# Moving layer two's memory attention to its beginning, twelve gates to its end, and eight state updates into the output stage

## The chip, the cores and the metric

The kernel runs on one core of one Trainium2 chip. A core has a matmul engine (TensorE, PE in the profile, with PEld for its weight loads), VectorE (DVE), ScalarE (ACT), GpSimd (POOL) and SyncE (SP), each with its own instruction queue, and 16 DMA engines that the queues of SP and POOL feed here. An engine runs its queue strictly in order. The metric is device time in microseconds (us) of one execution.

## What is computed

The reference is one inference step of a two-layer decoder trunk for 256 prompt tokens and 8 sample tokens (264 columns in all), width 2048. Layer one is sliding-window attention, layer two a gated linear recurrence (HGRN2) with 12 heads of key size 128 and value size 128. Each layer also has 4 memory heads. Both layers end in the same way:

```
branch = concatenate([mix, mem_o]) * silu(g)      # 12 mixer heads + 4 memory heads, 16 x 128
y = einsum('bte,ed->btd', branch, w_out_i)
return layer_norm(alpha * h + y)
```

In layer two the projection of the 264 tokens gives, for each head, a query q, a forget gate f and a value v, then 4 memory queries and 16 gate blocks g. For the prompt the recurrence runs over the tokens; for a sample token there is one step from a cached 128x128 state per head:

```
fg = lb + (1 - lb) * sigmoid(f);  k = 1 - fg;  q = silu(q)
o     = q . (fg * state) + (q . k) v
state = fg * state + k v^T                        # an output, per sample and head
o = o * rsqrt(mean(o^2) + eps) * norm_w
```

The memory heads attend to 256 memory rows: for the prompt, rows that the kernel projects itself, for each sample a cached set of keys and values (8 samples x 4 heads).

## The kernel before

All data stand with features on the 128 partitions and tokens in the free dimension. Every operand of a projection is split into two fp16 parts, a high and a low one, and a product is three matmuls (high-high, high-low, low-high: `passes`, L302 to L305). A 128-wide block of a projection (`proj`, L307) is thus 16 x 3 = 48 matmuls with 264 columns.

The program is a list of **units** (class `Stream`, L58). Most are a 1 MB block of weights (or of a cache) that SP loads into one of four `raw` slots (L79), ACT turns into its high half (L97), DVE into its low half (L98), in one of four `hl` slots; then the unit's function runs on PE. The loader and the splits run up to four units ahead. A unit that is not split, or is marked `whole`, keeps its raw slot until its own function has used it. Beside the list there is a queue of **sides**: generators for the work between projections, of which `pump(1)` advances the first by one step after each unit. A scheduler then fixes the order on each engine from the written order, its priorities and its own estimate of durations; an engine does not leave that order on the chip.

Names that the text below uses:

- `f`, `hv`, `hq`, `mq`, `g`, `o` are the outputs of projections: forget gate, value, query, memory query, gate, and output block.
- `hg_side` (L1064 to L1195) is the prompt's recurrence for a pair of heads. It runs over seven levels (1, 2, 4 up to 64): at each, ACT and DVE prepare a pair of split operands (L1079, L1080, L1084), PE makes products `hs` (12 matmuls), DVE keeps them under a mask (L1111). At the end come the transposes `pk` (L1152), ACT's copies `st` (L1147) and `kn` (L1154), the products `pu` (L1158) and `hpo` (L1169 to L1171), and the normalization: ACT squares, PE sums (`rms`, L1182), ACT takes a logarithm and an exponential with a table load before each (L1183, L1186), and DVE writes the head's `mix` (L1189). A gate (`gate_by`, L727 to L730) multiplies it by silu(g) and splits it for the output projection.
- `state_unit` (L1197) is the sample step of one head: eight small products with the cached state (`hos`), and the **state update**: eight matmuls `vb` (L1233) that spread the sample's v over the partitions, eight ACT scalings in place (L1237) and eight DVE multiply-adds in place (L1238), then POOL stores the 512 KB (L1241).
- `ck_unit`, `cv_unit` (outputs `mss`, `mso`) are the samples' memory attention, one unit per two samples for keys and for values; `memp_side` is the prompt's.

Layer two stands in this order: six pairs of heads, each with units f, f, v, v, q, state, q, state; in the first four pairs each head's gate follows its state unit (eight early gates, `NG1 = 8`); then four mq units; then the eight cache units with gates between them, the rest of the eight late gates; then 16 output units `o`. The first eight output units run over all 264 columns. The last eight have `held` slots of their own for the split weights and run over 176 columns first; the other 88 columns follow after the last of them, and then the final layer norm.

## Time and profile before

| what | value |
|---|---|
| runs | 905.26 us median of three (904.99 to 907.28) |
| profiled execution | 906.08 us, its span 904.3 us, granted TensorE clock 0.994 of full |
| PE busy | 886.6 us (98% of the span) |
| DVE busy | 701.5 us (78%) |
| ACT busy | 582.4 us (64%) |
| POOL busy | 34.9 us (4%) |
| DMA | 198.67 MB, 220 GB/s on average |

The span is from the first to the last instruction of one execution; the 1.8 us between it and that execution's time lie around it. PE counts as busy while a matmul is in flight, also when it runs at a lower clock, so a stage loses time in two ways: where PE is not busy, and where the granted clock is below 1. "Idle before, releaser" in a row is the time that the engine stood before that instruction and what ended it. For a group of instructions "busy us, mean ns" gives the union of their times and the mean of one. An instruction's own duration contains a fixed part that overlaps with the next one on the same engine, so the busy time divided by the count is what one of a row of them costs its engine.

### The profile page before, as it was taken

The page shows a single profiled execution, that of the slowest core. Times are in us where ns is not written, and L with a number is a line of the kernel's source. Part 1 is how long each engine was busy: PE and PEld are TensorE (multiplying, and loading weights), DVE is VectorE, ACT ScalarE, POOL GpSimd, SP SyncE. Part 2 cuts the span into 40 slices and gives each one's busy share as a digit, 9 for nine tenths or more (in the row PEclk, how much of TensorE's full clock was granted, in tenths as well). Part 3 has the DMA queues.
Part 4 walks back from the last instruction along what each step waited for, and adds up shares of the span by engine and source line. Part 5 has one row for each costly group of instructions (what it writes and reads, how often), then busy time and mean ns, then how long its engine had stood idle before and what let it go on. Part 6 is the DMA issues. An engine that isn't in the chain of part 4 may idle for free.

```text
span 904.3 us, 21814 instructions
## 1 busy us (share of the span) xinstructions
PE 886.6 (98%) x9281; PEld 762.9 (84%) x9281; DVE 701.5 (78%) x1230; ACT 582.4 (64%) x982; POOL 34.9 (4%) x68
## 2 busy tenths in 40 slices
PE   9999999999999999999999999999999999799996
PEld 6888889678888888876888888898888888688996
DVE  6879877669886666697687887979788989678736
ACT  6767776657664444476766877777777585858415
POOL 1100010000000000002000000000000000000000
PEclk9999999999999999999999999999999999899999
DMA  9998566557785555556374655827454878456303
GB/s 340 392 353 317 188 245 209 188 208 265 262 333 192 187 192 203 207 198 214 127 292 137 216 201 174 299 101 260 160 215 164 303 283 308 172 207 244 130 2 97
DMA packets 37853, 198.67 MB, mean 220 GB/s; under 512 B 4555, under 2 KB 10732, under 8 KB 17532
## 3 DMA queue, kind: packets, MB, share of 16 engines
q1 hardware_dynamic: 33024, 181.55, 56.3%
q0 software_dynamic: 4688, 15.67, 4.6%
q8 instruction: 72, 1.18, 0.5%
q14 instruction: 25, 0.20, 0.1%
q10 hardware_dynamic: 44, 0.07, 0.0%
HBM read 180.03 MB, written 17.22 MB: 218 GB/s over the span
## 4 chain that ended last, share of the span: by engine, by line
PE 77%; DVE 8%; ACT 6%; DMA 6%; issue 3%; SPq 0%; ACTq 0%; DVEq 0%
PE o L303 5%; PE o L305 5%; PE o L304 5%; PE g L305 5%; PE g L303 5%; PE g L304 5%; DVE hl L98 4%; ACT hl L97 2%; PE hv L305 2%; PE hv L303 2%; PE hv L304 2%; DMA raw<-in_w_in 2%; PE hq L303 2%; PE hq L305 2%; PE hq L304 2%
## 5 line engine op out<-in xcount | busy, mean ns | idle before, releaser
L98 DVE SCALAR_TENSOR_TENSOR hl<-raw,hl 128x2048 f16<-128x2048 f32 (+2 forms) x168 | 358.6, 2138 | 82.0 <-ACT hl L97 81.0
L97 ACT ACTIVATE hl<-raw 128x2048 f16<-128x2048 f32 (+2 forms) x168 | 299.2, 1784 | 97.8 <-PE o L305 45.4
L305 PEld LDWEIGHTS <-hl 128*128 128x128 f16 (+2 forms) x2048 | 197.4, 98 | 31.8 <-DVE hl L98 2.9
L303 PEld LDWEIGHTS <-hl 128*128 128x128 f16 (+2 forms) x2048 | 197.3, 98 | 30.6 <-issue 2.2
L304 PEld LDWEIGHTS <-hl 128*128 128x128 f16 (+2 forms) x2048 | 197.4, 98 | 30.3 <-issue 2.2
L305 PE MATMUL g<-xhl,hl 128*128 128x264 f16 x512 | 142.0, 277 | 2.4 <-DVE hl L98 2.4
L303 PE MATMUL g<-xhl,hl 128*128 128x264 f16 x512 | 141.9, 277 | 0.0
L304 PE MATMUL g<-xhl,hl 128*128 128x264 f16 x512 | 141.9, 277 | 0.0
L303 PE MATMUL o<-mix,hl 128*128 128x264 f16 x384 | 105.4, 276 | 0.8 <-DVE xres L747 0.8
L304 PE MATMUL o<-mix,hl 128*128 128x264 f16 x384 | 105.8, 276 | 0.0
L305 PE MATMUL o<-mix,hl 128*128 128x264 f16 x384 | 105.7, 276 | 0.0
L303 PE MATMUL q<-xhl,hl 128*128 128x264 f16 x192 | 53.0, 276 | 1.0 <-DVE kst L251 1.0
L303 PE MATMUL f<-xhl,hl 128*128 128x264 f16 x192 | 52.9, 276 | 0.4 <-DVE mvhl L251 0.4
L305 PE MATMUL hv<-xhl,hl 128*128 128x264 f16 x192 | 53.0, 276 | 0.0
L303 PE MATMUL hq<-xhl,hl 128*128 128x264 f16 x192 | 53.0, 276 | 0.0
L304 PE MATMUL hq<-xhl,hl 128*128 128x264 f16 x192 | 53.0, 276 | 0.0
L305 PE MATMUL hq<-xhl,hl 128*128 128x264 f16 x192 | 53.0, 276 | 0.0
L304 PE MATMUL hv<-xhl,hl 128*128 128x264 f16 x192 | 53.0, 276 | 0.0
L303 PE MATMUL hv<-xhl,hl 128*128 128x264 f16 x192 | 53.0, 276 | 0.0
L304 PE MATMUL q<-xhl,hl 128*128 128x264 f16 x192 | 53.0, 276 | 0.0
L305 PE MATMUL q<-xhl,hl 128*128 128x264 f16 x192 | 53.0, 276 | 0.0
L304 PE MATMUL f<-xhl,hl 128*128 128x264 f16 x192 | 52.9, 276 | 0.0
(338 smaller groups left out, 1858.4 us busy)
## 6 DMA issues: line engine op xcount, KB each, us to landing
raw<-in_w_in SPq DMA_DIRECT2D x88, 1024.0 KB, 6.4
raw<-in_w_o SPq DMA_DIRECT2D x32, 1024.0 KB, 5.0
raw<-in_w_mk SPq DMA_DIRECT2D x8, 1024.0 KB, 4.9
raw<-in_w_mv SPq DMA_DIRECT2D x8, 1024.0 KB, 4.9
raw<-in_c_mk SPq DMA_DIRECT2D x8, 1024.0 KB, 5.1
raw<-in_c_mv SPq DMA_DIRECT2D x8, 1024.0 KB, 7.0
raw<-in_state SPq DMA_DIRECT2D x12, 512.0 KB, 5.4
out_ss<-raw POOLq DMA_DIRECT2D x12, 512.0 KB, 5.5
```

The costliest lines, as they stand in the source:

```text
L97: hi = self.nc.scalar.activation(hl[:, 0, s], raw[:, s], AF.Copy, scale=scale)
L98: lo = self.nc.vector.scalar_tensor_tensor(hl[:, 1, s], raw[:, s], scale, hl[:, 0, s], op0=ALU.mult, op1=ALU.subtract)
L303: mm(out, lhs(0), rhs(0), start=start, stop=False)
L304: mm(out, lhs(0), rhs(1), start=False, stop=False)
L305: return mm(out, lhs(1), rhs(0), start=False, stop=stop)
```

## The change

- The four memory queries and the eight cache units come right behind the first f unit of layer two, mixed with the units of the first pair of heads. The prompt's memory attention is queued behind the last memory query.
- A pair has one state unit for its two heads, behind both q units. It loads the pair's 1 MB, and its small operations (products with q, their splits, the sum) run once for the pair. The factor 1/(SA*SK), which one DVE operation per head applied, is put into the constant `sel`.
- Early gates remain for heads 0, 2, 3 and 6. The other twelve come after the last pair, heads 10 and 11 at the very end.
- Heads 4 to 11 no longer update their state in the state unit. That unit stores what the update needs (v, fg and k, 320 bytes per partition and head) to DRAM (`kept`). Behind the output units 0, 2, 4 up to 14 stands an **update unit** each: it loads the head's 512 KB of state a second time, with its kept piece, into a raw slot, updates it and stores it. It isn't split, so it keeps its raw slot until its store has been made.
- From the first pair's state unit on, sides advance by two steps per unit where more than one waits.

The core of the diff:

```diff
--- before.py
+++ after.py
@@ -31,7 +31,8 @@
-NG1 = 8
+EARLY = (0, 2, 3, 6)
+LATER = tuple(range(4, HD))
...
+KEPT = P // 2 + 2 * TS
...
         n = 4 if i == 0 else 2 if i < 4 else 1
-        w = self.units[i][0].shape[1] // n
+        src = self.units[i][0]
+        if isinstance(src, list):
+            return [None]
+        w = src.shape[1] // n
         return [slice(k * w, (k + 1) * w) for k in range(n)]
 
     def load(self, i):
         t = self.pool.tile([P, 2048], F32, tag="raw", name=f"raw{i}", bufs=self.nraw)
         for k, s in enumerate(self.parts(i)):
+            if s is None:
+                for home, src in self.units[i][0]:
+                    self.nc.sync.dma_start(home(t), src)
+                continue
             self.nc.sync.dma_start(t[:, s], self.units[i][0][:, s])
             if i < 4:
                 self.after_load(i, k)
...
+    kept = {pi: dp.tile([P, 2, KEPT], F32, name=f"kept{pi}") for pi in sorted({h // 2 for h in LATER})}
...
-            nc.vector.tensor_scalar_mul(ks8, kk, 1.0 / (SA * SK))
...
-            scaled = mix[:, h] if h >= NG1 else sq
+            scaled = sq if h in EARLY else mix[:, h]
...
+    def update(h, R, vr, fgs, ks, sel):
+        for g in range(2):
+            pvb = bank("pt", 2, f"vb{h}{g}")
+            for bb in range(4):
+                mm(pvb[:, bb * P : (bb + 1) * P], sel[:, 4 * g + bb], vr, start=True, stop=True)
+            for bb in range(4):
+                b = 4 * g + bb
+                s = R[:, b]
+                nc.scalar.activation(s, s, AF.Copy, scale=fgs[:, b : b + 1])
+                nc.vector.scalar_tensor_tensor(
+                    s, pvb[:, bb * P : (bb + 1) * P], ks[:, b : b + 1], s, op0=ALU.mult, op1=ALU.add
+                )
+        nc.gpsimd.dma_start(ss_o[h // 2, :, h % 2 * TS * P : (h % 2 + 1) * TS * P], R.rearrange("p b v -> p (b v)"))
...
+    def update_unit(h):
+        def fn(raw):
+            if not late_sel:
+                late_sel.append(cp.tile([P, TS, P], F16, tag="ms", name="late_sel", bufs=2))
+                nc.sync.dma_start(late_sel[0], sel_d)
+            R = raw[:, : TS * P].rearrange("p (b v) -> p b v", b=TS)
+            k = raw[:, TS * P : TS * P + KEPT]
+            update(h, R, k[:, : P // 2].bitcast(F16), k[:, P // 2 : P // 2 + TS], k[:, P // 2 + TS :], late_sel[0])
+
...
+    def state_unit(pi):
         def fn(hl):
             p1 = H["p"]
-            pi, i = h // 2, h % 2
...
+            raw = stream.raw[state_at[pi]]
+            v = hl.rearrange("p s (i b v) -> p s i b v", i=2, b=TS)
+            vr, fgs, ks = cur["vr"], cur["fg"][:, :, TP:T], cur["kk"]
+            qs, vts = (cur[n][:, :, TP:T] for n in ("q", "vt"))
...
+            qkh = p1.tile([P, 2, 2, TS], F16, tag="qkh", name=f"qkh{pi}", bufs=2)
+            split_from(qfh[:, :, :, 0], qfh[:, :, :, 1], qf, 1.0)
+            split_from(qkh[:, 0], qkh[:, 1], qk, 1.0)
+            po = bank("ms", 1, f"hos{pi}")
+            pov = po[:, : 4 * TS].rearrange("p (i b s) -> p i b s", i=2, s=2)
+            for i in range(2):
+                for b in range(TS):
+                    mm(pov[:, i, b], v[:, 0, i, b], qfh[:, i, b], start=True, stop=False)
+                    mm(pov[:, i, b, 0:1], v[:, 1, i, b], qfh[:, i, b, 0:1], start=False, stop=True)
+            pq = po[:, 4 * TS : 6 * TS]
             for s in range(2):
-                mm(pq, H["ones"], qkh[:, s], start=s == 0, stop=s == 1)
+                mm(pq, H["ones"], qkh[:, s].rearrange("p i b -> p (i b)"), start=s == 0, stop=s == 1)
             nc.vector.tensor_reduce(qf, pov, axis=AX.X, op=ALU.add)
...
-            for g in range(2):
-                pvb = bank("pt", 2, f"vb{h}{g}")
-                for bb in range(4):
-                    mm(pvb[:, bb * P : (bb + 1) * P], H["sel"][:, 4 * g + bb], vr, start=True, stop=True)
-                for bb in range(4):
-                    b = 4 * g + bb
-                    s = R[:, b]
-                    nc.scalar.activation(s, s, AF.Copy, scale=fgs[:, b : b + 1])
-                    nc.vector.scalar_tensor_tensor(
-                        s, pvb[:, bb * P : (bb + 1) * P], ks8[:, b : b + 1], s, op0=ALU.mult, op1=ALU.add
-                    )
-            nc.gpsimd.dma_start(ss_o[pi, :, i * TS * P : (i + 1) * TS * P], raw)
+            nc.vector.tensor_tensor(qk, pq.rearrange("p (i b) -> p i b", i=2), vts, op=ALU.mult)
+            nc.vector.scalar_tensor_tensor(osb[pi][:, :, TP:T], qf, 1.0 / (SA * SA), qk, op0=ALU.mult, op1=ALU.add)
+            if 2 * pi in LATER:
+                tail = vr[:, :, P // 2 :]
+                nc.vector.tensor_copy(tail[:, :, :TS], fgs)
+                nc.vector.tensor_copy(tail[:, :, TS:], ks)
+                nc.gpsimd.dma_start(kept[pi], vr)
+                return
+            R = raw.rearrange("p (i b v) -> p i b v", i=2, b=TS)
+            for i in range(2):
+                update(2 * pi + i, R[:, i], vr[:, i, : P // 2].bitcast(F16), fgs[:, i], ks[:, i], H["sel"])
 
         return fn
 
...
+    w1("f", 0, f_unit(0))
+    for h in range(NM):
+        w1("mq", h, mem1_sides(mq_unit(h)) if h == NM - 1 else mq_unit(h))
+    cache(c_mk, ck_unit, 0)
+    w1("f", 1, f_unit(1))
+    cache(c_mk, ck_unit, 1)
+    cache(c_mk, ck_unit, 2)
+    w1("v", 0, hv_unit(0))
+    cache(c_mk, ck_unit, 3)
+    w1("v", 1, hv_unit(1))
+    w1("q", 0, hq_unit(0))
+    cache(c_mv, cv_unit, 0)
+    cache(c_mv, cv_unit, 1)
+    gate_of(0)
+    cache(c_mv, cv_unit, 2)
+    cache(c_mv, cv_unit, 3)
+    w1("q", 1, hq_unit(1))
+    state_of(0)
+    for pi in range(1, HD // 2):
         for part, unit in (("f", f_unit), ("v", hv_unit)):
             for i in range(2):
-                stream.add(wb(w_in1, NB1[part] + 2 * pi + i), unit(2 * pi + i))
+                w1(part, 2 * pi + i, unit(2 * pi + i))
+        w1("q", 2 * pi, hq_unit(2 * pi))
+        w1("q", 2 * pi + 1, hq_unit(2 * pi + 1))
+        state_of(pi)
         for h in (2 * pi, 2 * pi + 1):
-            stream.add(wb(w_in1, NB1["q"] + h), hq_unit(h))
-            state_at[h] = len(stream.units)
-            stream.add(state[pi][:, (h % 2) * TS * P : (h % 2 + 1) * TS * P], state_unit(h), SA, whole=True)
-            if h < NG1:
-                stream.add(wb(w_in1, NB1["g"] + h), early_gate(h))
-    for h in range(NM):
-        stream.add(wb(w_in1, NB1["mq"] + h), mq_unit(h))
-
...
-    def g1(j):
-        stream.add(wb(w_in1, NB1["g"] + j), gate_unit(1, j))
-
-    late = deque(range(NG1, NC))
-    for n, (c, unit, t) in enumerate([(c_mk, ck_unit, t) for t in range(4)] + [(c_mv, cv_unit, t) for t in range(4)]):
-        stream.add(c[1, t], unit(1, t), SA)
-        if late and (late[0] < NQ or n == 7 or late[0] < NQ + 2 and n > 3):
-            g1(late.popleft())
-    while late:
-        g1(late.popleft())
+            if h in EARLY:
+                gate_of(h)
+    last = (HD - 2, HD - 1)
+    for j in [j for j in range(NC) if j not in EARLY and j not in last] + list(last):
+        gate_of(j)
     for i in range(NC):
         stream.add(wb(w_o[1], i), out_unit(1, i), home=hold if i >= NC - NSPLIT else None)
+        if i % 2 == 0 and i // 2 < len(LATER):
+            h = LATER[i // 2]
+            srcs = [
+                (lambda t: t[:, : TS * P], state[h // 2][:, (h % 2) * TS * P : (h % 2 + 1) * TS * P]),
+                (lambda t: t[:, TS * P : TS * P + KEPT], kept[h // 2][:, h % 2]),
+            ]
+            stream.add(srcs, update_unit(h), split=False)
...
-        pump(1)
+        pump(2 if len(side) > 1 and i > state_at[0] else 1)```

What stands on the engines at three places follows, the names as in the code, the numbers behind a name being the unit or the head. First, ACT at the end of the last pair's recurrence. Before:

```order
L97 ACTIVATE hl153_10922<-raw153_10651 128x2048
L1147 ACTIVATE st5_10088<-hs5_64_10507 64x4x64
L1154 ACTIVATE kn5_10526<-pk5_10521 128x512
L1162 ACTIVATE s15_10570<-pu5_10565 128x256
L672 ACTIVATE mrows1_10690,mrz1_10692<-mrow1_10687,mrnm1_10691 32x256
```

In the changed kernel, same place:

```order
L106 ACTIVATE hl155_11053<-raw155_11046 128x2048
L1087 ACTIVATE qk16_2_5659<-qk32_10_9550 128x2x4x64
L1155 ACTIVATE st5_10129<-hs5_64_10544 64x4x64
L1213 ACTIVATE raw157_11050<-raw157_11050 128x128 x7
L1162 ACTIVATE kn5_10563<-pk5_10558 128x512
L1213 ACTIVATE raw157_11050<-raw157_11050 128x128
L1170 ACTIVATE s15_10631<-pu5_10626 128x256
```

Seven scalings of head 6's state (raw157, an update unit's slot) have moved between the copies `st` and `kn`; the split of a weight block (hl155, output unit 3) stands ahead of `st`.

Second, PE at the same moment. Before, with the memory softmax and the gates behind it:

```order
L1152 MATMUL pk5_10521<-ident_66,qk32_10_9379 128x128 x4
L1169 MATMUL hpo5_10636<-st5_10088,vn10_9535 128x128
L1170 MATMUL hpo5_10636<-st5_10088,vn10_9535 128x128
L1158 MATMUL pu5_10565<-vn10_9535,kn5_10526 128x128 x4
L666 MATMUL mrow1_10687<-ident_66,mst1_10685 32x128 x2
...
L677 MATMUL mback1_10698<-ident_66,mrows1_10690 128x32 x2
L1182 MATMUL rms50_10704<-osq50_10644,ones_rms_81 128x264
L1182 MATMUL rms51_10707<-osq51_10646,ones_rms_81 128x264
```

In the changed kernel:

```order
L315 MATMUL o11_0_11056<-mix_99,hl152_10895 128x264
...
L1160 MATMUL pk5_10558<-ident_66,qk32_10_9550 128x128 x4
L1177 MATMUL hpo5_10697<-st5_10129,vn10_9705 128x128
L1178 MATMUL hpo5_10697<-st5_10129,vn10_9705 128x128
L1166 MATMUL pu5_10626<-vn10_9705,kn5_10563 128x128 x4
...
L1209 MATMUL vb50_11167<-raw154_10782,late_sel_11017 128x128
L1190 MATMUL rms50_10769<-osq50_10705,ones_rms_81 128x264
L1190 MATMUL rms51_10772<-osq51_10707,ones_rms_81 128x264
...
L1209 MATMUL vb61_11328<-raw157_11050,late_sel_11017 128x128
...
L313 MATMUL o10_0_10964<-mix_99,hl150_10779 128x264
```

The end of the recurrence has moved into the output stage (o10 and o11 are layer two's output units 0 and 1): 30 matmuls of each unit, its first ten of 16 blocks, stand ahead of it; from `pk` on only `hpo`, `pu`, `rms` and the 24 `vb` of three updates (heads 4, 5 and 6) follow, and then the output units' blocks 10 to 15, of which blocks 10 and 11 are this very pair's.

Third, SP's loads in the output stage. Before:

```order
L79 DMA raw161_11165<-in_w_o 128x2048
L79 DMA raw162_11241<-in_w_o 128x2048
L79 DMA raw163_11301<-in_w_o 128x2048
L79 DMA raw164_11367<-in_w_o 128x2048
L79 DMA raw165_11426<-in_w_o 128x2048
```

In the changed kernel:

```order
L88 DMA raw155_11046<-in_w_o 128x2048
L88 DMA raw156_11048<-in_w_o 128x2048
L86 DMA raw157_11050<-in_state 128x1024
L86 DMA raw157_11050<-kept3_94 128x80
L88 DMA raw158_11194<-in_w_o 128x2048
L88 DMA raw159_11196<-in_w_o 128x2048
L86 DMA raw160_11198<-in_state 128x1024
L86 DMA raw160_11198<-kept3_94 128x80
```

Between two blocks of weights each there is now a state with its kept piece, in the same queue and out of the same four raw slots.

61 lines of the change are left out of this document (24 added, 37 removed).

## The prediction

> **What bounds the kernel now.** I read the page's busy times first, then layer two stage by stage, then the timeline of the one stage that loses time.
>
> ```profile
> PE 886.6 (98%) x9281; PEld 762.9 (84%) x9281; DVE 701.5 (78%) x1230; ACT 582.4 (64%) x982; POOL 34.9 (4%) x68
> core 0: us, PE busy (x) PEld busy (x) DVE busy (x) ACT busy (x) POOL busy (x), PEclk, DMA share, GB/s
> 420.00:725.00 305.00, 304.64 (x3218) 269.81 (x3218) 251.97 (x489) 219.48 (x390) 14.69 (x27) 1.00 0.58 206
> 750.00:775.00 25.00, 22.33 (x253) 19.22 (x250) 22.31 (x28) 14.03 (x18) 0.40 (x1) 1.00 0.76 275
> 775.00:800.00 25.00, 22.17 (x264) 18.32 (x265) 20.39 (x37) 20.64 (x39) 0.15 (x1) 0.86 0.58 220
> 800.00:825.00 25.00, 24.70 (x221) 21.46 (x220) 17.04 (x25) 15.94 (x21) 0.00 (x0) 1.00 0.43 158
> 825.00:850.00 25.00, 24.52 (x233) 21.54 (x231) 23.27 (x20) 16.77 (x13) 0.00 (x0) 1.00 0.70 259
> ```
>
> PE bounds: in the recurrence's stage (420 to 725) it stands 0.36 us of 305, though DVE is busy for 83% of it. The losses are in the 50 us behind: 2.67 + 2.83 us of idle, and a clock of 0.86 over 25 us, worth 0.14 x 25 = 3.5 us. **That is 9.0 us; the output stage to 850 loses 0.30 + 0.48 = 0.8.** Taking DVE or ACT work out of 420 to 725 gains at most 0.4 us.
>
> The 9 us are the end of the last pair's recurrence, a chain from engine to engine:
>
> ```profile
> 769.31 0.63 PE L1152 MATMUL pk<-ident,qk 128*128 128x128 f32 x4
> 771.06 0.36 ACT L1147 ACTIVATE st<-hs 64x256 f32<-64x256 f32 x1
> 771.32 0.58 ACT L1154 ACTIVATE kn<-pk 128x512 f32<-128x512 f32 x1
> 771.47 0.49 PE L1169 MATMUL hpo<-st,vn 128*128 128x128 f32 x2 [1.53 <-ACT st L1147]
> 774.93 0.57 ACT L1173 ACTIVATE osb<-hpo 128x512 f32<-128x512 f32 x1
> 776.41 1.28 ACT L1183 ACT_TABLE_LOAD   x1
> 778.58 1.28 ACT L1186 ACT_TABLE_LOAD   x1
> 780.33 0.90 DVE L1189 SCALAR_TENSOR_TENSOR mix<-osb,small_t,osq 128x264 f32<-128x264 f32 x2 [3.67 <-ACT osq L1186]
> ```
>
> From `kn` to the end of the last `mix` it takes 781.23 - 771.32 = 9.9 us. Little independent PE work stood beside it.
>
> **Part by part.** Prices of what moves, and the spacing of PE's products:
>
> ```profile
> L1237 ACT ACTIVATE raw<-raw,fg 128x128 f32<-128x128 f32 x96 | 29.5, 391 | 3.5 <-DVE hl L98 3.5
> L1238 DVE SCALAR_TENSOR_TENSOR raw<-vb,ks,raw 128x128 f32<-128x128 f32 x96 | 26.7, 345 | 0.2 <-PE vb L1233 0.2
> L97 ACT ACTIVATE hl<-raw 128x2048 f16<-128x2048 f32 x69 | 131.3, 1905 | 25.5 <-DMA raw<-in_w_in 6.7 <-PE g L305 6.4 <-issue 3.8
> L98 DVE SCALAR_TENSOR_TENSOR hl<-raw,hl 128x2048 f16<-128x2048 f32 x69 | 158.0, 2292 | 23.9 <-ACT hl L97 23.4
> 808.44 0.28 PE L305 MATMUL o<-mix,hl 128*128 128x264 f16 x1
> 808.55 0.28 PE L303 MATMUL o<-mix,hl 128*128 128x264 f16 x1
> 854.79 0.24 PE L303 MATMUL o<-mix,held 128*128 128x176 f16 x1
> 854.86 0.24 PE L304 MATMUL o<-mix,held 128*128 128x176 f16 x1
> 721.92 0.39 PE L1169 MATMUL hpo<-st,vn 128*128 128x128 f32 x2
> 722.14 0.39 PE L1233 MATMUL vb<-vr,sel_t 128*128 128x128 f16 x4
> 722.37 0.44 PE L1170 MATMUL hpo<-st,vn 128*128 128x128 f32 x2
> 779.76 0.17 PE L696 MATMUL mso<-msphl,hl 128*128 128x2 f16 x1
> 779.78 0.17 PE L697 MATMUL mso<-msphl,hl 128*128 128x1 f16 x1
> ```
>
> One update costs ACT 8 x 29.5/96 = 2.5 us, DVE 8 x 26.7/96 = 2.2 us and PE 8 x 0.23/4 = 0.46 us. A block costs PE 48 x 0.1125 = 5.4 us at 264 columns (0.11 between starts) and 48 x 0.076 = 3.65 us at 176. An fp32 product starts every 0.11 us.
>
> *Sample steps by pairs.* 12 small products fewer at about 0.025 us: **-0.3 us**. Some 40 DVE and 20 ACT operations on 8 or 16 columns go too; they lay under PE work (the 304.64 of 305), so nothing. The updates of heads 4 to 11 leave that stage: 64 x 0.28 = 18 us of DVE and 20 us of ACT, again covered by PE.
>
> *Memory attention first.* Same products, same splits, a place without any recurrence beside it. The changed order runs the 128 value products `mso` in one go, 128 x 0.025 = 3.2 us, and behind them stands a projection whose split queues behind the last cache split: ACT 1.9 and twice DVE 2.29 make 6.5 us, from a slot that comes free about when `mso` starts. So PE waits 0 (slots free earlier) to 3 us. **+1.0 us**, nearer the low end, since transposes and an update's products stand between.
>
> *Twelve gates last.* They were to lie beside the last pair's recurrence, but in the order shown the end of the recurrence stands behind the first 60 matmuls of output units 0 and 1, and nothing but its own products and 24 `vb` stands behind it. Blocks 10 and 11 of the output projection are that pair's. So PE must stand through the chain again. From `pk`:
> - `kn` waits for seven scalings of head 6's state (7 x 0.31 = 2.15 us), and these for that state's load, issued once DVE has split output unit 3 out of the same slot. Three DVE operations, about 1.5 us, lie between that split and `pk`. State loads take:
>
> ```profile
> DMA to landing us min/median/max: 3.8/5.4/7.3
> ```
>
>  With 0.3 us for SP's issue the state lands 2.6 to 4.2 us after `pk`, or has landed if PE comes late. `kn` then starts 0.65 + 2.15 = 2.8 to 6.4 us after `pk`; I take 4.6, the middle. (Before: 2.0, behind a weight split.)
> - From `kn` to `mix` 9.9 us, less about 0.8 for the memory softmax's operations, which stood in that chain and are gone: 9.1.
> - Then the gate, three operations of 0.43, and four multiply-adds of an update ahead of it (1.1): 2.4.
>
> Sum 16.1 us. PE's own work in it: 24 fp32 products of 0.11 (2.6), `rms` 0.9, 24 `vb` 1.4, together 4.9. Idle 11.2 us (9.4 to 13.0). The clock cost 3.5 us around the old gap; for the new I take 2.0 (0 to 3.5), since `vb` lies spread through it. 13.2 us against 9.0: **+4.2 us** (+0.4 to +7.5).
>
> [...]
>
> *Updates in the output stage.* Their ACT and DVE time fits (for two blocks of 10.8 us DVE has 2 x 2.29 + 2.2 and some 2.5 of sums). The four raw slots are the question. Rows for the weight loads of this stage and for the stores of a state, from issue to landing:
>
> ```profile
> DMA to landing us min/median/max: 4.8/5.0/6.8
> DMA to landing us min/median/max: 2.9/5.5/7.4
> ```
>
> A state holds its slot until PE has come to its `vb` and the store has landed. Call R the moment at which PE resumes. PE then has 36 matmuls of units 0 and 1 (4.05 us) and five blocks (27) before head 7's `vb`: R+31.5. Update with other work about 3.2: R+34.7; store 5.5: R+40.2; in its slot the load of output unit 12, 5.0, and its split, 1.9 + 2.29: R+49.4; in that slot unit 13, again 9.2: R+58.6, where PE needs it at R+56.5 (one more wide block, five narrow ones, three updates' `vb`). In that slot head 11's state lands at R+64.0; its eight scalings stand on ACT ahead of unit 15's split (2.5 + 4.2): R+70.7, where PE needs unit 15 at R+64.25. So 6.4 us late with medians, and 1.8 with the fastest rows (2.9, 4.8, 3.8). I take the middle, 4.1, less the 0.8 that the stage loses now: **+3.3 us** (+1.0 to +5.6). The stores' traffic itself (8 states read again, 4 MB) isn't the bound: this stage's DMA share was 0.43 and 0.70.
>
> **Sum**: -0.3 + 1.0 + 4.2 + 3.3 = +8.2 us on the profiled execution's 906.08: 914.3; that execution is 0.8 us above the median of the runs: **913.5 us**.
>
> **Rivals.**
> 1. *The chain runs bare (faster).* Place: ACT between `st` and `kn`, decided by head 6's state landing before `pk`. Summing the chain's own rows instead of its distances, `kn` 0.6, `pu` 1.1, copy 0.4, `hpo` 1.1, 0.6, 0.7, table 1.3, 0.9, table 1.3, 0.4, `mix` 0.9 and gate 1.3 give 10.6; with 0.65 + 2.15 ahead 13.4, less PE's 4.9: 8.5, and `vb` keeps the clock up. And the loader's lead of up to eight held blocks takes the output stage's 0.8 to 0, the recurrence's 0.4 goes: 8.5 - 9.0 - 0.8 - 0.4 - 0.3 = -2.0; if two of the links overlap by another 1.5, -3.5: **902 us**. For it: ACT has slack there. Against: the 9.9 us measured is the longer reading, and the slot order above.
> 2. *The gap only moves (no change).* The gap's 9.4 with a clock as now or better, loads at their fastest: +0.4 + 1.0 - 0.3: **906 us**. For it: the same chain made the old gap.
> 3. *The recurrence lags PE's order throughout (much slower).* A late pair now has six blocks, 32.4 us, and some 8 us of its own products per pass, but
>
> ```profile
> 493.57 0.44 PE pk L1152 x4
> 545.25 0.49 PE pk L1152 x4
> ```
>
>  one pass took 51.7 us with eight blocks. If passes need 45 us instead of 40.4, four of them cost 18 us: **925 us**. Against: DVE loses 18 us of updates there, and the order keeps a recurrence running behind several units.
>
> **Chances.** Forecast (907 to 921) 0.60; rival 1 0.18; rival 2 0.15; rival 3 0.07. The forecast's own range is the sum of the bounds, 906.5 to 921; toward rival 1 the range goes to 901. What a measurement of this kernel can tell from no change is about 0.3%, 2.7 us: faster 0.18, same 0.18, slower 0.64.
>
> **What would show it.** In the new profile the old losses at 750 to 800 are gone from the gates' stage; PE stands some 10 us in `hpo` and the first resumed `o`, released by ACT `kn` and DVE L740, with a clock below 1 around it; ACT L1213 waits for in_state; late `o<-mix,held` rows wait for DVE L107 behind in_w_o. It is wrong if that gap is under 7 us, if no held block waits, or if `hs` products wait over 5 us in the pairs' stage.

## The result and the profile after

| kernel | runs | ratio to before |
|---|---|---|
| before | 905.48 us median of four (904.99 to 907.28) | |
| after | 920.43 us median of four (918.53 to 922.76) | 1.0157, 95% interval 1.0136 to 1.0179 |

The change makes the kernel 14 us slower (0.0157 x 905.48 = 14.2). The forecast was slower, 913.5 us, with a range of 901 to 921. The profiled execution of the changed kernel took 922.76 us, its span 921.0 us, 16.7 us more than the 904.3 before. That execution is the slowest of the four, 2.3 us above their median.

The page's busy times come first:

```profile
PE 894.4 (97%) x9269; PEld 768.2 (83%) x9269; DVE 696.3 (76%) x1178; ACT 581.7 (63%) x964; POOL 37.2 (4%) x72
```

PE is busy 7.8 us longer than before (894.4 against 886.6) with twelve instructions fewer, and idle 8.9 us longer (921.0 - 894.4 = 26.6, against 904.3 - 886.6 = 17.7). So about half of the loss is idle time, and the other half is the same products at a lower clock (0.984 of full over the span, against 0.994). The windows (width, then busy time of PE, PEld, DVE, ACT and POOL, then the granted clock) show where, first after and then before:

```profile
475.00:500.00 25.00, 24.39 (x298) 20.73 (x297) 18.33 (x19) 17.10 (x27) 0.00 (x0) 0.86 0.67 232
700.00:840.00 140.00, 130.95 (x1262) 112.81 (x1261) 102.47 (x177) 90.53 (x147) 4.32 (x8) 0.96 0.49 169
840.00:895.00 55.00, 50.52 (x576) 48.17 (x574) 38.37 (x83) 25.73 (x47) 2.67 (x5) 0.94 0.57 211
```

```profile
475.00:500.00 25.00, 25.00 (x269) 22.27 (x267) 19.58 (x33) 16.47 (x37) 0.00 (x0) 1.00 0.43 153
700.00:840.00 140.00, 134.16 (x1458) 116.50 (x1456) 117.65 (x177) 95.41 (x122) 2.15 (x4) 0.98 0.70 255
840.00:895.00 55.00, 54.52 (x851) 53.10 (x850) 31.60 (x71) 20.06 (x45) 0.00 (x0) 1.00 0.15 51
```

Idle time plus (1 - clock) x width is what a stage loses. (The clock is printed to 0.01, so the figure is good to 0.7 us over 140 us and to 0.3 over 55.)

| stage | before | after | more |
|---|---|---|---|
| memory attention first, 475 to 500 | 0 | 0.6 + 3.5 = 4.1 | 4.1 |
| end of the last recurrence, 700 to 840 | 5.8 + 2.8 = 8.6 | 9.0 + 5.6 = 14.6 | 6.0 |
| held output blocks, 840 to 895 | 0.5 | 4.5 + 3.3 = 7.8 | 7.3 |

The three sum to 17.4, against 16.7 in the spans. Each has its chain of rows.

**The end of the last recurrence.** PE's timeline and ACT's in the changed kernel:

```profile
797.72 0.63 PE L1160 MATMUL pk<-ident,qk 128*128 128x128 f32 x4
802.04 1.46 PE L1166 MATMUL pu<-vn,kn 128*128 128x128 f32 x8 [2.98 <-ACT kn L1162]
814.16 0.60 PE L313 MATMUL o<-mix,hl 128*128 128x264 f16 x2 [3.99 <-ACT mix L739]
```

```profile
799.36 2.15 ACT L1213 ACTIVATE raw<-raw 128x128 f32<-128x128 f32 x7 [1.06 <-DMA raw<-kept]
801.41 0.57 ACT L1162 ACTIVATE kn<-pk 128x512 f32<-128x512 f32 x1
811.38 0.90 DVE L1197 SCALAR_TENSOR_TENSOR mix<-osb,small_t,osq 128x264 f32<-128x264 f32 x2 [0.61 <-ACT osq L1194]
```

`kn` comes 3.7 us behind `pk`. ACT first waits for head 6's kept piece, then does its seven scalings. From the start of `kn` to the start of `mix` it takes 10.0 us, and from there to the first resumed product of output unit 0 another 2.8: 16.4 us from `pk`, with little for PE to do.

**The held output blocks.** SP's waits between 820 and 900, then DVE's timeline, then PE's:

```profile
SPq L86 <- DMA out_ss<-raw: 8.4, 1, 8.4
SPq L88 <- DMA out_ss<-raw: 6.2, 1, 6.2
```

```profile
848.57 2.29 DVE L107 SCALAR_TENSOR_TENSOR held<-raw,held 128x2048 f16<-128x2048 f32 x1
857.72 2.29 DVE L107 SCALAR_TENSOR_TENSOR held<-raw,held 128x2048 f16<-128x2048 f32 x1 [2.69 <-ACT held L106]
859.92 0.42 DVE L757 SCALAR_TENSOR_TENSOR xres<-xres,o 128x264 f32<-128x264 f32 x1
885.51 2.29 DVE L107 SCALAR_TENSOR_TENSOR held<-raw,held 128x2048 f16<-128x2048 f32 x1 [1.45 <-ACT held L106]
```

```profile
860.40 0.24 PE L313 MATMUL o<-mix,held 128*128 128x176 f16 x1 [2.33 <-DVE xres L757]
887.87 0.25 PE L315 MATMUL o<-mix,held 128*128 128x176 f16 x1 [2.00 <-DVE held L107]
```

Loads wait 6.2 and 8.4 us for a state's store to leave its raw slot. By the ring of slots, three of the four held the states of heads 7, 8 and 9, so the weights of output units 10 and 11 went one after the other through the fourth: the split of unit 10 ended at 850.86, unit 11's load was issued at 850.89. Its split stood on DVE from 857.72 for 2.29 us, and the sum of output unit 7 (`xres`), next in DVE's order, started behind it at 859.92. That sum empties the accumulation bank that output unit 9 needs: PE stood 2.33 us, though unit 9's own weights had long been split. At 887.87 output unit 15 waits for its own split.

**The clock.** The stretches that the trace shows at half clock, three of them with the 3.41 us ahead:

```profile
485.32:488.73 3.41, 3.41 (x108) 3.38 (x106) 1.53 (x1) 3.41 (x5) 0.00 (x0) 1.00 0.51 216
488.73:495.56 6.83, 6.22 (x64) 4.61 (x61) 6.83 (x8) 5.26 (x5) 0.00 (x0) 0.50 0.71 217
802.75:806.16 3.41, 3.36 (x21) 2.97 (x19) 1.64 (x6) 0.46 (x2) 0.26 (x1) 0.50 0.00 0
812.99:819.82 6.83, 5.66 (x26) 3.74 (x26) 2.21 (x7) 1.36 (x3) 0.53 (x1) 0.50 0.94 350
857.37:860.78 3.41, 1.07 (x18) 0.95 (x16) 3.03 (x3) 0.65 (x2) 0.00 (x0) 1.00 0.65 223
860.78:864.19 3.41, 3.41 (x27) 3.41 (x25) 3.29 (x13) 2.28 (x3) 0.00 (x0) 0.50 0.68 254
884.67:888.08 3.41, 1.26 (x17) 0.88 (x15) 2.56 (x3) 1.05 (x2) 0.00 (x0) 1.00 0.02 7
888.08:891.50 3.42, 3.42 (x27) 3.42 (x25) 2.80 (x11) 0.35 (x1) 0.53 (x1) 0.50 0.00 0
```

Each of the two windows of 3.41 us in which PE was busy 1.07 and 1.26 us is followed by one at half clock. So was the one ahead of 488.73, in which PE was busy throughout, 97 of its 108 products having one or two columns. The rows at 802.75 and 812.99 belong to the end of the last recurrence. In the first, products of the chain itself run at half clock and fill time in which PE would have waited; in the second, the resumed products of the output units do, and there the slow clock costs time.

### The profile page after: what moved, and what is told of

It is laid out like the page before. It is cut to its first block, busy times and chain, and to the rows that moved or that the text cites. A ratio compares the mean times of both kernels' runs of the same rounds, so it can differ in the third digit from the quotient of the medians.

```text
span 921.0 us, 21766 instructions
## 1 busy us (share of the span) xinstructions
PE 894.4 (97%) x9269; PEld 768.2 (83%) x9269; DVE 696.3 (76%) x1178; ACT 581.7 (63%) x964; POOL 37.2 (4%) x72
## 4 chain that ended last, share of the span: by engine, by line
PE 85%; ACT 5%; DMA 4%; DVE 4%; SPq 1%; issue 0%; ACTq 0%
PE g L313 6%; PE g L314 6%; PE g L315 6%; PE o L313 5%; PE o L315 5%; PE o L314 5%; PE f L313 2%; PE q L313 2%; PE f L314 2%; PE f L315 2%; PE q L315 2%; PE q L314 2%; PE hv L315 2%; PE hv L314 2%; PE hv L313 2%; PE hq L313 2%
## 5 line engine op out<-in xcount | busy, mean ns | idle before, releaser
L107 DVE SCALAR_TENSOR_TENSOR hl<-raw,hl 128x2048 f16<-128x2048 f32 (+2 forms) x162 | 357.6, 2210 | 100.6 <-ACT hl L106 99.8
L106 ACT ACTIVATE hl<-raw 128x2048 f16<-128x2048 f32 (+2 forms) x162 | 297.8, 1844 | 99.6 <-PE o L315 47.7
L313 PEld LDWEIGHTS <-hl 128*128 128x128 f16 (+2 forms) x2048 | 197.7, 98 | 36.8 <-issue 7.6
L315 PEld LDWEIGHTS <-hl 128*128 128x128 f16 (+2 forms) x2048 | 197.9, 98 | 29.5 <-issue 0.2
L313 PE MATMUL g<-xhl,hl 128*128 128x264 f16 x512 | 141.3, 276 | 0.3 <-DVE sil L744 0.3
L315 PE MATMUL g<-xhl,hl 128*128 128x264 f16 x512 | 141.3, 276 | 0.0
L313 PE MATMUL o<-mix,hl 128*128 128x264 f16 x384 | 106.9, 279 | 4.0 <-ACT mix L739 4.0
L314 PE MATMUL o<-mix,hl 128*128 128x264 f16 x384 | 107.2, 279 | 0.0
L315 PE MATMUL o<-mix,hl 128*128 128x264 f16 x384 | 107.1, 279 | 0.0
L313 PE MATMUL q<-xhl,hl 128*128 128x264 f16 x192 | 53.0, 276 | 2.1 <-DVE kst L261 2.1
L314 PE MATMUL hq<-xhl,hl 128*128 128x264 f16 x192 | 53.7, 280 | 0.0
L313 PE MATMUL hq<-xhl,hl 128*128 128x264 f16 x192 | 53.7, 280 | 0.0
L315 PE MATMUL hq<-xhl,hl 128*128 128x264 f16 x192 | 53.6, 279 | 0.0
L313 PE MATMUL f<-xhl,hl 128*128 128x264 f16 x192 | 53.0, 276 | 0.4 <-DVE mvhl L261 0.4
L315 PE MATMUL q<-xhl,hl 128*128 128x264 f16 x192 | 53.0, 276 | 0.0
L313 PE MATMUL hv<-xhl,hl 128*128 128x264 f16 x192 | 53.0, 276 | 0.0
L315 PE MATMUL hv<-xhl,hl 128*128 128x264 f16 x192 | 53.0, 276 | 0.0
L315 PE MATMUL f<-xhl,hl 128*128 128x264 f16 x192 | 53.0, 276 | 0.0
```

What stands on the lines that cost most here:

```text
L106: hi = self.nc.scalar.activation(hl[:, 0, s], raw[:, s], AF.Copy, scale=scale)
L107: lo = self.nc.vector.scalar_tensor_tensor(hl[:, 1, s], raw[:, s], scale, hl[:, 0, s], op0=ALU.mult, op1=ALU.subtract)
L313: mm(out, lhs(0), rhs(0), start=start, stop=False)
L314: mm(out, lhs(0), rhs(1), start=False, stop=False)
L315: return mm(out, lhs(1), rhs(0), start=False, stop=stop)
```

## The experiments

Lost time is read as above throughout. Most kernels are the changed one with an edit; two are the kernel before with one part of the change (twelve late gates; sample steps by pairs). The kernel before had medians of 905.74 to 906.46 us beside them.

### Updates at home

```diff
-LATER = tuple(range(4, HD))
+LATER = ()
```

> All twelve heads update their state in the pair's state unit, as before the change; no update unit stands in the output stage. Memory first, twelve late gates and the sample steps by pairs stay as changed. Theory (the changed kernel lost its time by place: 3.6 us around 475 to 500, 14.3 against 9.0 us around the end of the last recurrence, 8.4 against 0.8 us in two waits of held output blocks): the two held-block waits go, -7.6 us, and kn stands about 2 us behind pk again instead of 3.7, -1.7 us; the clock dip near 489 stays. 920.4 - 9.3 = 911, within 909 to 913. Rival (the updates slow the recurrence where they stand beside it: 18 us of DVE and 20 us of ACT return there): the end of the last recurrence comes 3 to 9 us later, and the time is 914 to 920.

Measured: 915.59 us, ratio 1.0101 (1.0073 to 1.0130).

```profile
700.00:725.00 25.00, 20.74 (x180) 17.91 (x176) 13.55 (x36) 16.47 (x37) 1.61 (x3) 0.86 0.34 128
840.00:895.00 55.00, 55.00 (x721) 52.50 (x720) 34.63 (x58) 18.85 (x27) 0.00 (x0) 1.00 0.25 95
```

```profile
698.55 4.78 ACT L1213 ACTIVATE raw<-raw,fg 128x128 f32<-128x128 f32 x16 [1.84 <-DVE hl L107]
703.24 1.89 ACT L106 ACTIVATE hl<-raw 128x2048 f16<-128x2048 f32 x1
808.74 0.60 ACT L1162 ACTIVATE kn<-pk 128x512 f32<-128x512 f32 x1
```

The held blocks lose nothing, and `kn` stands 0.67 us behind its `pk` (808.07) instead of 3.7: both parts of the theory hold. But 7.8 us appear at 700 to 725, where nothing was lost before. A pair's sixteen scalings stand in one piece on ACT, 4.78 us, ahead of a weight split and of that pair's own `st` and `kn`. The time lies in the rival's range. The rival had the right engine and the wrong place: not a slower recurrence all along, but one stall. Taking the updates out of the pairs' stage does buy something; it is lost again at the held blocks.

### Own slots for four updates

```diff
+        if self.units[i][6] == "hl":
+            t = self.pool.tile([P, 2, 2048], F16, tag="hl", name=f"ust{i}", bufs=self.nsplit)
+            t = t.rearrange("p s c -> p (s c)").bitcast(F32)
+        else:
             t = self.pool.tile([P, 2048], F32, tag="raw", name=f"raw{i}", bufs=self.nraw)
...
-            stream.add(srcs, update_unit(h), split=False)
+            stream.add(srcs, update_unit(h), split=False, home="hl" if h >= 8 else None)
```

The loader also counts these four as it counts a split block, so it doesn't stop at them.

> The changed kernel, but the update units of heads 8 to 11 load their state into slots of the split ring, which the held output blocks leave unused, and no longer into the four raw slots; the loader doesn't wait for them. Theory (the held blocks wait for raw slots that an update holds until its store has landed): the waits of 2.5 and 2.2 us at held blocks and the half-clock stretches behind them go, 8.4 us to under 2: 920.4 - 7 = 913, within 911 to 916. Rival (the held blocks wait because ACT and DVE are in order, with eight scalings that wait for a state and a kept piece ahead of the split): the same waits stay, 919 to 921.

Measured: 914.54 us, ratio 1.0085 (1.0052 to 1.0117).

```profile
840.00:895.00 55.00, 53.99 (x765) 51.95 (x763) 45.39 (x100) 27.50 (x53) 2.65 (x5) 1.00 0.47 179
```

The held blocks lose 1.0 us instead of 7.8, and SP no longer waits for a state's store, where it had waited 8.4 and 6.2 us. The scalings are as many and as long as before, 2.45 us for eight. But the scheduler dealt the order of ACT and DVE anew here (head 8's scalings, for one, now stand ahead of splits that they stood behind), so this run speaks for the shortage of slots and doesn't rule out the rival by itself.

### The same without the late stores

The store at the end of `update` is left out for heads 4 to 10.

> The changed kernel, but the update units of heads 4 to 10 don't store their state (the new states of these heads are left out of the output); head 11's does. Theory (a raw slot is held until the store has landed, a median of 3.4 us behind the last multiply-add): each slot comes free 3.4 us or more earlier, the two waits at held blocks go from 8.4 us with their slow clock to under 4: 920.4 - 5 = 915, within 912 to 917. Rival (the slot is held by the early load, which then waits for PE to come to the update's products, and the store adds little): the waits stay over 6 us, 918 to 921.

Measured: 912.22 us, ratio 1.0081 (1.0055 to 1.0106).

```profile
840.00:895.00 55.00, 54.99 (x819) 53.24 (x818) 41.90 (x98) 27.21 (x58) 0.54 (x1) 1.00 0.38 135
```

With the stores gone the loss is gone, although the states are loaded, held and updated as in the changed kernel. PE's order is that of the changed kernel, though parts of ACT's and DVE's are not. Against the rival of the run before stands one row of ACT: its scalings (`raw`, L1213) still wait for a kept piece, 2.1 us at the longest, and no held block is late for it. The stores' traffic isn't the cause either, since the weight loads land after a median of 4.9 us in both kernels. What tips the ring over is the store's share of the hold, a median of 3.4 us from issue to landing in the changed kernel.

### Value caches later

```diff
-    cache(c_mv, cv_unit, 0)
-    cache(c_mv, cv_unit, 1)
     gate_of(0)
-    cache(c_mv, cv_unit, 2)
-    cache(c_mv, cv_unit, 3)
...
                 w1(part, 2 * pi + i, unit(2 * pi + i))
+                if pi == 1:
+                    cache(c_mv, cv_unit, 2 * (part == "v") + i)
```

> The changed kernel, but the four value-cache units stand among the f and v units of the second pair, not among those of the first. Two places are read apart. Around 475 to 500: theory (the 128 products with one or two columns in one go, and the 0.8 us behind them, bring the half clock of 488.7 to 495.6): no half-clock stretch and under 1 us lost there, -3 us; rival (the dip belongs to the chain of transposes and softmax or to the start of the recurrence, not to the run of small products): a dip of about 3 us stays at that place. Around 790 to 825: theory (the recurrence of the six pairs is one serial chain of about 50 us a pair, which memory first started late): pair one's recurrence starts four units, 21 us, earlier, pair two has four units more, so the chain ends 10 us earlier or so and the stand of 9.4 us before the resumed output products shrinks to under 4; rival: it stays at 9. Both theories: 908 to 912; only the first: 917.

Measured: 919.39 us, ratio 1.0134 (1.0100 to 1.0168).

```profile
475.00:525.00 50.00, 48.51 (x608) 42.55 (x607) 40.24 (x65) 36.44 (x60) 1.08 (x2) 1.00 0.64 232
700.00:840.00 140.00, 131.17 (x1266) 113.19 (x1265) 103.10 (x171) 91.74 (x148) 3.23 (x6) 0.96 0.50 177
```

The time fell by 1.0 us only, where 917 was expected for the first theory alone. The dip is gone with the run of small products: clock 1.00, and 1.5 us of idle over 50 us in place of 4.1 in 25. The second theory fell. The first pair's recurrence began four units earlier, yet 700 to 840 lost 8.8 + 5.6 = 14.4 us as before. PE did not come to `pk` late because the recurrence was late: in the changed kernel's trace no product `hs` waits as much as half a microsecond. PE comes to `pk` where its fixed order puts it, behind the 60 products of output units 0 and 1, and only from there on is the chain bare. The theory that took its place: the loss is made by what PE's order puts beside the chain from `pk` to `mix`. The run with the memory units spread over the pairs, below, tests it.

### Order of the chunks in an output block

```diff
-        for c in range(NC):
-            passes(pt[:, :n], ..., c == 0, c == NC - 1)
+        order = [*range(HD - 2), *range(HD, NC), HD - 2, HD - 1] if name[:2] == "o1" else range(NC)
+        for c in order:
+            passes(pt[:, :n], ..., c == order[0], c == order[-1])
```

> The changed kernel, but each output block of layer two multiplies the chunks of the memory heads (12 to 15) before those of the last pair (10, 11), so 42 instead of 30 products of each of the first two output units can run before the last pair is done. Theory: 24 products of 0.1125 us, 2.7 us, move from behind the stand into it: 920.4 - 2.7 = 917.7, and the stand of 9.4 us is 6 to 7. Rival (PE reaches pk later, everything of the chain behind pk hangs on pk, and the stand only moves by the same amount): 920, the stand still 9.

Measured: 916.47 us, ratio 1.0107 (1.0079 to 1.0135).

```profile
475.00:500.00 25.00, 23.25 (x309) 20.46 (x308) 18.52 (x23) 18.19 (x31) 0.00 (x0) 1.00 0.63 230
```

```profile
488.64 0.18 PE L708 MATMUL mso<-msphl,hl 128*128 128x1 f16 x1 [0.65 <-DVE hl L107]
491.91 0.29 PE L315 MATMUL hq<-xhl,hl 128*128 128x264 f16 x1 [1.10 <-DVE hl L107]
...
800.82 0.49 PE L1178 MATMUL hpo<-st,vn 128*128 128x128 f32 x2 [1.01 <-ACT st L1156]
812.21 0.60 PE L313 MATMUL o<-mix,hl 128*128 128x264 f16 x2 [4.00 <-ACT mix L740]
```

The last rows show what the 24 products did: PE reaches the chain later, head 6's state has landed and been scaled by then, and the 2.98 us in front of `pu` become 1.01 in front of `hpo`. The 4.0 us in front of the resumed block stay, since they hang on `mix`. Over the whole chain the stands of PE shrink from 8.3 to 6.6 us, as the theory said, and not by nothing, as the rival did. The time fell by 4.0 us, 1.3 more than the products weigh. In this execution the memory stage shows no half clock, and yet loses 0.65 + 1.10 = 1.75 us, the waits for late splits. Where the half clock comes, it hides a part of them (0.6 us idle in the changed kernel).

### Memory spread over the pairs

```diff
-    w1("f", 0, f_unit(0))
-    for h in range(NM):
-        w1("mq", h, mem1_sides(mq_unit(h)) if h == NM - 1 else mq_unit(h))
...
+    beside = {
+        1: [lambda h=h: mq1(h) for h in (0, 1)],
+        2: [lambda h=h: mq1(h) for h in (2, 3)],
+        3: [lambda t=t: cache(c_mk, ck_unit, t) for t in range(4)],
+        4: [lambda t=t: cache(c_mv, cv_unit, t) for t in range(4)],
+    }
...
-EARLY = (0, 2, 3, 6)
+EARLY = ()
```

> The changed kernel with another order of units: the first pair's units come first, the twelve memory units stand two or four at a time beside the units of pairs two to five, and all sixteen gates stand behind the last pair. Late updates and sample steps by pairs stay. In PE's order the last pair's pk, pu, hpo and rms now stand among the products of late gates 13 to 15, with two whole gate blocks behind them, before the first output unit. Theory (the stand of 9.4 us and the slow clock around it, 14.3 us in all, are an effect of PE's order, which left the chain from pk to mix without cover): under 2 us lost between 700 and 825, no 128 small products in one go, so under 1.5 us at the memory stage as well, and the 8 us at held blocks stay: 920.4 - 12.5 - 2.5 = 905, within 903 to 909. Rival (the recurrence needs some 50 us a pair whatever stands beside it, so PE waits in the products hs instead): waits of 5 us or more in the pairs' stage, 912 to 920.

Measured: 913.88 us, ratio 1.0087 (1.0070 to 1.0104).

```profile
700.00:840.00 140.00, 139.08 (x1365) 121.77 (x1364) 104.90 (x174) 88.98 (x140) 3.24 (x6) 1.00 0.53 190
840.00:895.00 55.00, 46.45 (x710) 45.37 (x708) 39.33 (x87) 26.91 (x52) 2.67 (x5) 0.97 0.50 181
```

With the same chain, the same products and the same late updates, but gate products beside the chain and two whole gate blocks behind it, 700 to 840 loses 0.9 us instead of 14.6. So the loss there is one of PE's order. The late scalings no longer stand in that chain either; that can be worth no more than the 4 us by which the run with updates at home lost less there (10.6 against 14.6), so most of the term is the missing cover. The time is another matter: 913.88 misses the theory's range of 903 to 909 and lies in the rival's. The rival's waits at `hs` are small (0.3 us), but between 630 and 700 PE stands 4.0 us, 1.2 to 1.4 us each ahead of `hvp`, `hpo` and `mso`, where the changed kernel lost 0.2 in all of 500 to 700. And the held blocks lose 8.6 + 1.7 = 10.2 us instead of 7.8. That PE now reaches them without having stood, and that the stand had hidden a part of the shortage of slots, is the likely reason; it isn't shown by itself.

### Three mends together

The order just told, the order of the chunks, and the own slots.

> The order of units of the run with the memory units spread over the pairs, the chunks of the memory heads ahead of the last pair's in each output block, and the update units of heads 8 to 11 in slots of the split ring. Theory (the three places add up): lost between 700 and 825 under 2 us, at held blocks under 2 us, at the memory stage under 1.5 us: 920.4 - 12.5 - 7 - 2.5 = 898, within 895 to 902, faster than before the change. Rival (a loss mended in one place turns up in the next, since the same loads and the same recurrence come later): 904 or more.

Measured: 906.70 us, ratio 1.0006 (0.9994 to 1.0019), over ten runs.

```profile
700.00:840.00 140.00, 139.65 (x1375) 122.47 (x1374) 103.98 (x165) 90.86 (x141) 3.24 (x6) 1.00 0.55 196
840.00:895.00 55.00, 51.24 (x821) 49.31 (x818) 45.92 (x116) 31.66 (x71) 2.67 (x5) 1.00 0.52 193
```

The end of the recurrence loses 0.4 us. The held blocks still lose 3.8: heads 4 to 7 have no own slots. The 4.0 us between 630 and 700 are there as in the run before. So the three places don't add up as the theory had it, and the time lies in the rival's range, 8.7 us above the theory's 898. This kernel is the same as the one before the change within what can be told.

### Memory first with the gates and updates of before

`EARLY = tuple(range(8))` and `LATER = ()` in the changed kernel, head 1's gate behind the first state unit.

> Memory first and the sample steps by pairs, but eight early gates beside the first four pairs as before the change, eight late gates, and all state updates in the pair's state unit. In PE's order the last pair's products hs of the last two levels and everything behind them stand behind the pieces of output units 0 and 1, with nothing between them. Theory (twelve late gates are what keeps memory first from exposing more of the recurrence): the products of two more levels lie bare, some 3 us each, so the stand is 6 us longer than the 10.5 us lost there with updates at home: 915.6 + 6 = 921.6, within 918 to 926. Rival (late gates give nothing, the loss is the late updates' and the pairs' stage gains from blocks beside it): 910 or less.

Measured: 914.20 us, ratio 1.0101 (1.0076 to 1.0126).

```profile
700.00:840.00 140.00, 131.10 (x1311) 114.18 (x1310) 108.83 (x189) 90.80 (x137) 3.77 (x7) 0.95 0.53 191
```

Here 700 to 840 loses 8.9 + 7.0 = 15.9 us. Over 725 to 840 the kernel with updates at home, which has four more late gates, lost 6.0 idle with a clock of 0.96, 10.6 in all. The 5 us between them are close to the 6 expected for two bare levels. The time of 914.20 lies between the two ranges, as the stall of 7.8 us at 700 does not occur in this order. So twelve late gates help memory first by some 5 us at this place, but in the total the kernel with updates at home, with its stall, is 1.4 us slower than this one.

### Twelve late gates in the kernel before

```diff
-NG1 = 8
+NG1 = 4
```

> The kernel before the change with four early gates instead of eight, so twelve late ones; memory at its old place behind the pairs, state updates and sample steps as before. In PE's order the last pair's pk to rms now stand among the products of late gate 14, the prompt's memory attention behind them. Theory (late gates as such are no loss: they cover the end of the recurrence): the 9.0 us lost between 750 and 800 before shrink to 0 to 5, 905.5 - 6 = 899.5, within 897 to 903. Rival (with seven blocks and 16 scalings beside each pair instead of nine the recurrence lags PE's order): 906 to 914, with waits at hs or at hvp in the pairs' stage.

Measured: 915.52 us, ratio 1.0104 (1.0089 to 1.0120).

```profile
700.00:840.00 140.00, 131.86 (x1423) 113.56 (x1421) 112.55 (x162) 91.21 (x123) 1.09 (x2) 0.95 0.61 223
```

```profile
793.86 1.85 PE L1182 MATMUL rms<-osq,ones_rms 128*128 128x264 f32 x4 [1.14 <-ACT osq L1177]
801.74 0.37 PE L303 MATMUL msc<-mkhl,mqhl 128*128 128x256 f16 x1 [3.53 <-ACT ms L614]
```

The theory failed, and the fault lay in the reading of the order: late gate 14 ends before `pk`, and behind `rms` stand the four score products of the prompt's memory attention (`msc`) with no gate between. The rival's waits aren't there either: `hs` waits 1.5 us in the whole run. The chain is as bare as in the changed kernel, and a second chain, the memory's softmax (3.53 us), follows it: 8.1 + 7.0 = 15.1 us. In the kernel before, the samples' 128 value products and late gate 14 filled this place. More late gates are no cover by themselves; only those are that stand behind `pk` in PE's order.

### Updates beside the gates

The three mends, with the update units of heads 4 to 7 behind late gates 0, 3, 6 and 9.

> The run with the three mends, and besides the update units of heads 4 to 7 stand behind late gates 0, 3, 6 and 9 instead of behind output units 0, 2, 4 and 6; those of heads 8 to 11 stay in the split ring's slots behind output units 8, 10, 12 and 14. Theory (what the output stage still lost there, 2.6 us idle at 843.6, 1.0 at 854.3 and the slower products between, 4.3 in all, is a raw slot held by one of these four updates): the output stage loses under 1 us, and the gates, whose DVE and ACT are free a third of the time, lose nothing: 906.7 - 4 = 902.7, within 900 to 905. Rival (the scalings and multiply-adds stand in front of the last pairs' recurrence on ACT and DVE): waits of 3 us or more at hs or pk between 730 and 780, 906 or more.

Measured: **903.91 us, ratio 0.9974 (0.9965 to 0.9984)**, over nine runs.

```profile
700.00:840.00 140.00, 137.22 (x1348) 119.64 (x1346) 112.69 (x174) 92.53 (x132) 3.77 (x7) 1.00 0.66 238
840.00:895.00 55.00, 53.58 (x843) 51.59 (x840) 38.01 (x108) 24.82 (x67) 2.74 (x6) 1.00 0.28 101
```

The time is the theory's, its places only in part: the held blocks lose 1.4 us (under 1 was expected), and the gates' stage 2.8 instead of 0.4 (nothing was expected). The rival is out, as no wait there is longer than 1.7 us. This kernel is 2.4 us faster than the one before the change (0.0026 x 906), and the only one that beats it.

### Updates beside later gates

The same with gates 2, 5, 8 and 13.

> As the run with updates beside the gates, with the four update units behind gates 2, 5, 8 and 13, so that the last two fall beside the end of the last recurrence. Theory (place is free as long as no raw slot is held in the output stage): the same time within 2 us, 901 to 905. Rival (scalings ahead of kn on ACT lengthen the last chain, as in the changed kernel): 2 to 4 us longer, with PE standing before the first output unit.

Measured: 906.96 us, ratio 1.0003 (0.9990 to 1.0016), 3 us more.

```profile
678.12 2.44 ACT L1218 ACTIVATE raw<-raw 128x128 f32<-128x128 f32 x8 [0.65 <-DMA raw<-kept]
680.47 0.36 ACT L1175 ACTIVATE s<-pu 128x256 f32<-128x256 f32 x1
```

The rival holds, at another place than it named. Eight scalings landed on ACT ahead of `s` at the end of the fifth pair's recurrence, and PE's `hpo` waited 4.1 us for it. So the four updates cost some 2.4 us beside the gates, and at these later places, one of them ahead of a chain, 3 us more.

### Sample steps by pairs in the kernel before

The state unit of the changed kernel with `LATER = ()`, `EARLY = tuple(range(8))`, memory, gates and `pump(1)` as before.

> The kernel before with one part of the change: one state unit and one set of sample steps for each pair of heads. Memory behind the pairs, eight early and eight late gates and one step of the sides a unit, as before the change; all state updates in the state units. Theory (the sixteen scalings of a pair now stand in one go on ACT, 4.8 us, ahead of a weight split, as in the run with updates at home, where PE stood 4.3 us at 701 and ran slowly behind it): one or more stands of over 2 us between 425 and 725, and in PE's order the prompt's msc products stand right behind rms with nothing between; 908 to 916. Rival (the part is worth its twelve products and hides the rest): 904.5 to 906.5, and no stand over 1 us in the pairs' stage.

Measured: 915.15 us, ratio 1.0099 (1.0083 to 1.0116). The profiled execution was 4.7 us above this median.

```profile
700.00:840.00 140.00, 129.55 (x1387) 111.19 (x1386) 111.62 (x173) 87.48 (x119) 2.16 (x4) 0.91 0.58 214
```

```profile
788.26 0.66 PE L1160 MATMUL pk<-ident,qk 128*128 128x128 f32 x4 [2.01 <-DVE qk L1092]
803.45 0.37 PE L313 MATMUL msc<-mkhl,mqhl 128*128 128x256 f16 x1 [3.67 <-ACT ms L624]
```

The time is the theory's, the place only half. No stand over 2 us in the pairs' stage; the loss is again at the end of the last recurrence, 10.5 + 12.6 = 23 us in this execution. All 128 value products now stand ahead of the last `hs`, so `rms` and `msc` are bare as with the twelve late gates. What the sixteen scalings have to do with that isn't shown.

## Why the prediction was right, and where its terms were not

The direction and the range held, the range narrowly: the median is 0.6 us below its upper end of 921, and two of the four runs lie above it. The sum, +8.2 us on the profiled execution, was half of the +16.7 measured. Two of its three larger terms lie outside their own bounds, and the profiled execution's +16.7 is above the sum of all the upper bounds, +15.8; the median lies inside because two of the executions were 4 us faster. So far the range held by luck. By its steps:

- **Sample steps by pairs, -0.3.** In the changed kernel nothing speaks against it. "So nothing" for the rest was too simple: the same edit alone in the kernel before costs 9 us. There `rms` and `msc` stand bare in PE's order, which speaks for an order dealt anew as the reason; no run shows that by itself.
- **Memory first, +1.0, bounds 0 to 3: measured 4.1.** The idle time was as told: 0.6 us here, 1.75 where the clock stayed up, and the late split was its cause. The step that failed was to price the 128 products at 0.025 us each and stop there. Behind them the clock was down for 6.8 us, 3.5 us of loss. With the products in portions of 32 it was 1.00 over 475 to 525.
- **Twelve gates last, 13.2 us against 9.0: measured 14.6 against 8.6.** The chain is as long as worked, in part by luck. Between the prediction's own marks (`pk`, `kn`, end of the last `mix`, resumed product) it measures 3.7 + 10.9 + 1.9 = 16.4 us against 4.6 + 9.1 + 2.4 = 16.1: the middle link came out 1.8 us too short in the sum, the two others 1.4 too long. The late updates lengthened it, as told: with updates at home `pk` to the resumed product takes 11.3 us, and 3.0 of the 5.1 between lie ahead of `kn` (3.7 against 0.67). Idle was smaller than forecast, 9.0 us against 11.2, and the clock's part larger, 5.6 against 2.0: products of the chain ran at half clock and filled time that would have been idle, and the resumed products ran at half clock for 6.8 us. That `vb` keeps the clock up, as the term of 2.0 us and the first rival had it, no run shows.
- **Updates in the output stage, +3.3, bounds 1.0 to 5.6: measured +7.3.** The mechanism was right: raw slots held until a store has landed. SP's waits show it, and the loss goes away both when four updates get slots of their own and when the stores are left out. The idle part agrees, 4.5 us against 4.1, but half of it by luck. The predicted chain of loads, from unit 12 to unit 15, ends in the 2.00 us at unit 15. The other 2.33 come by a link that was missing: the sum of output unit 7 waits on DVE behind unit 11's split, so a late load stops PE two units earlier than the unit it was for. The loads and stores of the states, for their part, landed faster than assumed (medians of 3.9 and 3.4 us instead of 5.4 and 5.5). Mis-sized was the clock: behind each of the two stands came 3.4 us at half clock, some 1.7 us, and the term had none.
- **The rivals.** The bare chain that ends faster, and the gap that only moves, did not occur. The recurrence did not lag PE's order either.
- **The signs named beforehand** showed, two of them with another detail: the old losses left the gates' stage; PE stood 8.3 us instead of some 10, behind `kn` at `pu` and not at `hpo`, and the resumed `o` was released by the gate's operation on ACT (L739) and not on DVE; ACT's scalings waited for head 6's load; and of the two late held products one waited for DVE L107 behind `in_w_o`, the other for a sum of output unit 7 that stood behind it.

Put by kind, the forecast's idle time was about right and its clock was not. It had +9.7 us of idle time (with the product count's -0.3) and -1.5 us of clock (2.0 against 3.5 before); measured were +7.8 us of idle time (0.6 + 3.2 + 4.0) and +9.6 us of clock (3.5 + 2.8 + 3.3). So the stages that lose were right, and in the main the chains in them, and the term that was mis-sized is the slow clock, which stood in the sum at one place out of three. In the changed kernel's trace the half-clock stretches before 900 us are 3.41 or 6.83 us long, and their starts at 488.73, 802.75, 812.99, 860.78 and 888.08 lie 314.02, 10.24, 47.79 and 27.30 us apart: 10.24 is three times 3.413, and the others are 92, 14 and 8 times that.

## What to carry to other kernels

An order that is fixed at build time decides what covers a long chain: read the engine's order from the first link of the chain to its consumer and count the independent products between, since work that stands merely before it or after it covers nothing. A buffer that an operation holds until its store has landed belongs in a ring of its own, or it starves the loads that share it (they waited 8.4 and 6.2 us here); and a late operand stops what stands behind it in its engine's order, not only its own user (PE stood 2.33 us at output unit 9, behind the split of unit 11). A stand of PE of two microseconds can cost twice, once as idle time and once by a slow clock after it: in the changed kernel's trace a half clock began within, or less than 1 us behind, four of the five stands of 2.0 to 4.0 us, and none at the fifth, of 2.13 us.
